# Second MLP's last quarter as seven half products with the final norm at its blocks, and the sum of four weight blocks built by loads in the lone steps

## Chip, core and metric

The kernel runs on one core of one Trainium2 chip. The time is in device microseconds (us), the median of several executions of the whole program. The engines are TensorE (PE), VectorE (DVE), ScalarE (ACT), GpSimd (POOL) and SyncE (SP). SP and POOL here mostly issue DMA transfers, each in the order of its own queue.

## What is computed

A trunk of two layers for 512 tokens with 1024 features. Each layer is a token mixer and a squared-ReLU MLP, and a last RMSNorm follows:

```
def sq_relu_mlp(h, w_up, w_down):
    return jnp.square(jax.nn.relu(h @ w_up)) @ w_down
...
    for i in range(DEPTH):
        h = rms_norm(x, norm_mix[i])
...
        h = rms_norm(x, norm_ffn[i])
        x = x + sq_relu_mlp(h, ffn_w_up[i], ffn_w_down[i])
    return rms_norm(x, final_norm)
```

`w_up` is 1024x4096 and `w_down` 4096x1024, all in float32.

## The kernel before

**The products.** A float32 product is made of three matmuls with operands split in two parts, high and low (`mm3`): high by high, high by low, low by high. The high part is a cast on ACT (L125), the low part a subtraction on DVE (L122). In the listings `wh` and `wl` are the two parts of a weight block (512x512), and a left operand is a pair of tiles `q`.

**The MLP.** `ffn` runs the hidden width in four quarters, c = 0 to 3. `up(c)` makes the squared hidden values of a quarter, four tiles `a11`, `a12`, `a21`, `a22` (`sq`). `down(c, sq)` multiplies them by the four blocks of `w_down` and adds the result to `x`. Either is a 2x2 product of blocks done by Winograd's scheme: seven half products instead of eight, each with a sum of weight blocks on one side. So one of `down`'s items has 2 x 4 x 3 = 24 matmuls with 512 columns, for the two 128-row blocks b = 0 and 1 of its half of the tokens. The items stand in a list `work` of pairs (prepare, go). `go` issues the matmuls of an item and then adds the two blocks to `x` on DVE (`accumulate`, L1155). `prepare` brings the weights, splits them and splits the left operand. The loop calls `prepare` of item j + 2 after `go` of item j. `up(c)` and `down(c - 1)` alternate, item by item. The last quarter has no partner: in the first MLP its seven items, `down(3)`, run by themselves. These are the **lone steps**, here numbered 1 to 7 as they run. Steps 1, 5, 6 and 7 use one pair of PSUM banks (X), and steps 5, 6 and 7 follow one another there. Since each adds to what the one before left, a block of step 6 or 7 can't start before DVE has read that bank.

**Weights of a lone step.** Six slots (`raws`) hold raw weight blocks. SP loads a block, and POOL adds another one to it during a transfer (`add`, L990, `accum_op`). With W00, W01, W10, W11 for the blocks of the last quarter, slot f has W00 for step 1, a has W01 + W00 for step 3, c has W10 for step 2, b has W11 for step 4. DVE then makes a = a + b for step 5 (`t2`, L1264). After that POOL adds W01 to b, which is the weight of step 6 (`p3`), and W10 to a, the sum of four, which is that of step 7 (`p4`).

**The end of the second MLP.** It gets `last_products` as `last`, and `down(3)` is not used. The four weight blocks are loaded and split whole, and eight plain half products follow (`block`, 24 matmuls each; the last one as two with 256 columns). After a block, DVE adds it to `x` (L1819), ACT sums the squares (L1823), DVE and POOL make the inverse root (L1829, L1837). For row blocks 0 to 2 `finish` scales the row of 1024 (L1842) and SP writes it out. For block 3 the product with the norm's gain is made ahead (L1862), and its two halves are scaled on DVE (L1867) and ACT (L1868).

A scheduler fixes the order of each engine's instructions when the program is built. On the chip each engine runs its own list in order and waits on semaphores.

Of the kernel before, what the change touches and what calls it, by code (L numbers as in the profile page):

```python
# [10 lines left out]
F32 = mybir.dt.float32  # L11
F32R = mybir.dt.float32r
# [5 lines left out]
P = 128  # L18
T = 512
NT = T // P  # L20
# [37 lines left out]
def trunk(ctx: ExitStack, tc: tile.TileContext, a):  # L58
# [10 lines left out]
    def nm(s):  # L69
        count[0] += 1  # L70
        return f"{s}_{count[0]}"
# [3 lines left out]
    def psum():  # L75
        if fixed[0] is not None:
            return fixed[0]()
        return psp.tile([P, T], F32, tag="ps", name=nm("ps"))
# [11 lines left out]
    def raw_tile(shape, name="wr"):  # L90
        return wp.tile(list(shape), F32, tag="wr", name=nm(name), bufs=2)
# [14 lines left out]
    def mm3(out, l, r, start, stop, terms=(0, 1, 2), **kw):  # L106
        (lh, ll), (rh, rl) = l, r
        for t in terms:
            lhsT, rhs = ((lh, rh), (lh, rl), (ll, rh))[t]
            nc.tensor.matmul(  # L110
                out, lhsT=lhsT, rhs=rhs, start=start and t == 0, stop=stop and t == 2, **kw
            )

    def gpair(t=None):

        if t is None:
            t = gxp.tile([P, 4, T // 2], F32R, tag="g", name=nm("g"))
        t = t.rearrange("p k n -> p (k n)")
        return t[:, 0:T], t[:, T : 2 * T]
# [4 lines left out]
    def split(hl, src, eng=None):  # L124
        nc.scalar.copy(hl[0], src)  # L125
        low(eng or nc.vector, hl[1], src, hl[0])
        return hl
# [20 lines left out]
    def wtiles(n1, n2, shift=0):  # L148

        return tuple(  # L150
            wp.tile([P, 2112], F32R, tag=t, name=nm(t))[:, shift : shift + n1 * n2].rearrange(
                "p (k c) -> p k c", k=n1
            )
            for t in ("wh", "wl")
        )
# [7 lines left out]
    def wview(w, r0, rows, c0, cols):  # L163
        return w[r0 : r0 + rows, c0 : c0 + cols].rearrange("(k p) c -> p k c", p=P)
# [87 lines left out]
    class Norm:  # L252
# [7 lines left out]
        def add(self, i, u):  # L260

            if u != self.late:
                self.square(i, u)
            else:
                self.left.append((i, u))
# [24 lines left out]
    def four(dtype=F32R):  # L290
        return gxp.tile([P, 4, H], dtype, tag="g", name=nm("g"))
# [697 lines left out]
    def add(t, src):  # L989
        nc.gpsimd.dma_start(t, src, accum_op=ALU.add)  # L990

    def ffn(layer, xq, norm, pool, after=None, last=None, mid=None):

# [162 lines left out]
        def down(c, sq):  # L1159
# [3 lines left out]
            def w(k, u):  # L1163
                return wview(w_dn, c * 1024 + k * 512, 512, u * 512, 512)
# [30 lines left out]
                return "a"  # L1195

            def p3():
                add(s["b"], w(0, 1))
                return "b"

            def p4():
                add(s["a"], w(1, 0))
                return "a"

            def n1():
                sq["n1"] = squares.get()
# [55 lines left out]

            def t2():
                nc.vector.tensor_add(s["a"], s["a"], s["b"])  # L1264

            return [
                item(lambda: "a11", w11, "X", True, (0, 0, r2, False), alone),
                item(lambda: "a12", w21, "Z", True, (0, 0, r2, True), True),
                item(n1, p1, "Y", True, (1, 1, nr2, False)),
                item(s4, w22, "Y", False, (0, 1, nr2, False), False, True, t2),  # L1270
                item(lambda: "a11", p2, "X", False, (0, 1, nr2, True), False, True),
                item(lambda: "a21", p3, "X", False, (1, 1, nr2, True), True, True),
                item(
                    lambda: "a22", p4, "X", False, (1, 0, r2, True), True, True,
# [8 lines left out]
                work += [p, q]  # L1283
            sq = new
        n_mixed = len(work)
        if last is None:
            work += down(3, sq)
        ahead = 2
        for prepare, _ in work[:ahead]:
            prepare()  # L1290
        for j, (_, go) in enumerate(work):
# [6 lines left out]
            go()  # L1298
            if j + ahead < len(work):
                work[j + ahead][0]()  # L1300
        if last is not None:
            spare[:] = banks
            last(
                r2,
                [
                    split(
                        (four(), four()) if n < 2 else tuple(
                            pool.tile([P, 4, H], F32R, tag="q", name=nm("q"), bufs=4)
                            for _ in range(2)
                        ), sq[t],  # L1310
                    )
                    for n, t in enumerate(("a11", "a12", "a21", "a22"))
                ],
            )
        fixed[0] = None


    norm1 = Norm(0)
    gx1 = Quarters("norm_mix", KD, 1)
    with stage(1), tc.tile_pool(name="ffn0", bufs=1) as fp:  # L1320
        ffn(0, gx0, norm, fp, norm1.add, None, gx1.first)

# [460 lines left out]
    with stage(1), tc.tile_pool(name="ffn1", bufs=1) as fp:  # L1785
        out = a["out"].rearrange("b (i p) d -> p (b i) d", p=P)

        def last_products(r2, quarters):
            w_dn = a["ffn_w_down"][1]
            ws = {}  # L1790
            gb = four(F32).rearrange("p k n -> p (k n)")
            for u in range(2):
                for kh in range(2):
                    raw = raw_tile((P, 4, 512))
                    nc.sync.dma_start(raw, wview(w_dn, 3 * 1024 + kh * 512, 512, u * 512, 512))
                    if u + kh < 2:
                        wh, wl = split(wtiles(4, 512), raw)
                        parts = [(wh[:, k, :], wl[:, k, :]) for k in range(4)]
                    else:
                        parts = [split(gpair(G6[k]), raw[:, k, :]) for k in range(4)]  # L1800
                    for k in range(4):
                        ws[u, kh * 4 + k] = parts[k]

            nc.sync.dma_start(gb, a["final_norm"].partition_broadcast(P))
            ssum = fp.tile([P, 16, 4], F32, name="ssum")

            def block(i, c0, cols, e):

                ps = psum()[:, 0:cols]
                bs = slice(i % 2 * P, (i % 2 + 1) * P)  # L1810
                u, w0 = c0 // 512, c0 % 512
                for k in range(8):
                    h, l = quarters[i // 2 * 2 + k // 4]
                    mm3(
                        ps, (h[:, k % 4, bs], l[:, k % 4, bs]),
                        tuple(t[:, w0 : w0 + cols] for t in ws[u, k]), k == 0, k == 7,
                    )
                yy = x[:, i, c0 : c0 + cols]
                nc.vector.scalar_tensor_tensor(  # L1819
                    out=yy, in0=ps, scalar=r2[:, i : i + 1], in1=yy, op0=ALU.mult, op1=ALU.add  # L1820
                )
                junk = tmp()
                nc.scalar.activation(  # L1823
                    junk[:, 0:cols], yy, AF.Square, accum_out=ssum[:, i, e : e + 1]
                )

            def mean(i, e, rest):
                m = small(1)
                nc.vector.tensor_scalar(  # L1829
                    out=m, in0=ssum[:, i, e : e + 1], scalar1=1.0 / D, scalar2=rest,  # L1830
                    op0=ALU.mult, op1=ALU.add,
                )
                return m

            def inverse(m):
                r = small(1)
                nc.gpsimd.tensor_tensor(out=r, in0=m, in1=mhalf[:, 0:1], op=ALU.pow)  # L1837
                return r

            def finish(i):  # L1840
                r = inverse(mean(i, 1, mean(i, 0, EPS)))
                nc.vector.scalar_tensor_tensor(  # L1842
                    out=x[:, i, :], in0=x[:, i, :], scalar=r, in1=gb, op0=ALU.mult, op1=ALU.mult,
                )
                nc.sync.dma_start(out[:, i, :], x[:, i, :])

            for i in range(0, 2):
                block(i, 0, 512, 0)
            for i in range(0, 2):
                block(i, 512, 512, 1)  # L1850
                finish(i)
            block(2, 0, 512, 0)
            block(2, 512, 512, 1)
            finish(2)

            i = NT - 1
            z = gpair(four(F32))
            m = EPS
            for e, (c0, cols) in enumerate(((0, 512), (512, 256), (768, 256))):
                block(i, c0, cols, e)  # L1860
                m = mean(i, e, m)
                nc.vector.tensor_mul(  # L1862
                    z[c0 // 512][:, c0 % 512 : c0 % 512 + cols], x[:, i, c0 : c0 + cols],
                    gb[:, c0 : c0 + cols],
                )
            r = inverse(m)
            nc.vector.tensor_scalar(out=z[1], in0=z[1], scalar1=r, scalar2=None, op0=ALU.mult)  # L1867
            nc.scalar.activation(z[0], z[0], AF.Copy, scale=r)  # L1868
            for uo in (1, 0):
                nc.sync.dma_start(out[:, i, uo * 512 : (uo + 1) * 512], z[uo])  # L1870

        ffn(1, gx2, norm2, fp, None, last_products)


_INS = [
# [22 lines left out]
```

## Time and profile before

| | us |
|---|---|
| median of 3 runs | 1098.06 (1094.0 to 1098.29) |
| the profiled execution's own time | 1092.22 |
| its span, first to last instruction | 1090.5 |
| TensorE busy in the span | 1058.8 |
| mean granted clock of TensorE, share of 2.4 GHz | 0.989 |

The span is cut from the profiled execution. Its own time is 1.72 us longer and stands 5.84 us under the median of the runs. Times in the rows below are us from the span's start.

### The profile page before, as it was taken

What the parts mean: (1) busy time and instruction counts of PE and PEld (TensorE: products, weight loads), DVE (VectorE), ACT (ScalarE), POOL (GpSimd) and SP (SyncE); (2) the same over time, 40 slices, a digit from 0 to 9 for tenths busy, and PEclk for the clock granted to TensorE, in tenths of its full rate; (3) what the DMA queues carried; (4) which work ended last, traced back from release to release, by engine and by line L of the source; (5) the groups of instructions that cost most, each with busy time, mean ns of one, the idle gap of its engine ahead of it and who ended that gap; (6) DMA issues with size and microseconds to landing.
All of it is one profiled execution on the core that took longest, in us unless ns stands there. A gap on an engine that the chain in (4) does not pass through costs nothing.

```text
span 1090.5 us, 15740 instructions
## 1 busy us (share of the span) xinstructions
PE 1058.8 (97%) x6540; PEld 947.4 (87%) x6540; DVE 864.3 (79%) x959; ACT 627.8 (58%) x712; POOL 115.4 (11%) x143
## 2 busy tenths in 40 slices
PE   8989999899999999989999999999999999999997
PEld 6778889899999999877788999887999899999986
DVE  6888866887887887887968588997988788888753
ACT  4567546665655655556755645556765555656531
POOL 5100000001001001002011000010001001001000
PEclk9989999999999999999999999999999999999999
DMA  6120246768768669447486836876686886757421
GB/s 204 39 79 2 76 117 197 204 142 174 212 144 186 178 149 199 149 78 175 139 161 141 231 85 193 237 134 181 156 222 125 218 194 125 225 115 119 120 109 59
DMA packets 86083, 163.33 MB, mean 150 GB/s; under 512 B 4917, under 2 KB 10620, under 8 KB 85884
## 3 DMA queue, kind: packets, MB, share of 16 engines
q0 software_dynamic: 33584, 67.11, 35.3%
q1 hardware_dynamic: 52428, 95.22, 25.4%
q8 instruction: 51, 0.84, 0.3%
q14 instruction: 20, 0.16, 0.0%
HBM read 160.22 MB, written 2.10 MB: 149 GB/s over the span
## 4 chain that ended last, share of the span: by engine, by line
PE 79%; DVE 8%; DMA 4%; issue 4%; ACT 4%; SPq 0%; POOL 0%; POOLq 0%; ACTq 0%; DVEq 0%
PE ps L110 74%; DVE wl L122 3%; ACT wh L125 2%; DMA wb<-in_sgu_w_in 2%; DMA wb<-in_ffn_w_down 1%; DVE g L122 1%; PE ps L1613 1%; PE ps L852 1%; DMA wb<-in_ffn_w_up 1%; PE ps L296 1%; PE ps L819 0%; PE ps L820 0%; PE ps L821 0%; PE ps L823 0%; PE ps L822 0%
## 5 line engine op out<-in xcount | busy, mean ns | idle before, releaser
L110 PE MATMUL ps<-g,wh 128*128 128x256 f32 (+1 forms) x2304 | 420.5, 285 | 9.0 <-DVE g L122 5.0
L110 PEld LDWEIGHTS ps<-g,wh 128*128 128x128 f32 x2304 | 359.9, 190 | 17.2 <-DVE g L122 5.9
L110 PE MATMUL ps<-g,wl 128*128 128x256 f32 (+1 forms) x1152 | 327.1, 284 | 0.6 <-DVE wl L122 0.6
L110 PE MATMUL ps<-wh,q 128*128 128x512 f32 (+1 forms) x840 | 266.5, 390 | 2.9 <-DVE x L1155 2.9
L122 DVE TENSOR_TENSOR wl<-wb,wh 128x2048 fp32r<-128x2048 f32 x75 | 171.7, 2289 | 68.8 <-ACT wh L125 68.8
L110 PEld LDWEIGHTS ps<-g,wl 128*128 128x128 f32 x1152 | 217.4, 189 | 2.2 <-DVE wl L122 0.9
L125 ACT CAST wh<-wb 128x2048 fp32r<-128x2048 f32 x75 | 143.0, 1907 | 119.5 <-PE ps L110 92.0
L110 PEld LDWEIGHTS ps<-wh,q 128*128 128x128 f32 x840 | 158.1, 189 | 34.9 <-issue 3.3
L122 DVE TENSOR_TENSOR wl<-wr,wh 128x2048 fp32r<-128x2048 f32 (+1 forms) x69 | 153.3, 2225 | 38.5 <-ACT wh L125 38.4
L125 ACT CAST wh<-wr 128x2048 fp32r<-128x2048 f32 (+1 forms) x69 | 127.8, 1855 | 64.2 <-PE ps L110 44.8
L110 PE MATMUL ps<-wl,q 128*128 128x512 f32 (+1 forms) x420 | 163.7, 390 | 0.0
L110 PE MATMUL ps<-wh,g 128*128 128x512 f32 x496 | 157.5, 395 | 1.9 <-DVE g L122 1.3
L110 PEld LDWEIGHTS ps<-wh,g 128*128 128x128 f32 x496 | 93.8, 189 | 23.3 <-DVE g L122 1.7
L125 ACT CAST q<-sq 128x1024 fp32r<-128x1024 f32 x51 | 53.6, 1051 | 90.4 <-PE ps L110 87.8
L110 PE MATMUL ps<-wl,g 128*128 128x512 f32 x248 | 97.7, 394 | 1.7 <-DVE wl L122 1.7
L110 PEld LDWEIGHTS ps<-wl,q 128*128 128x128 f32 x420 | 79.5, 189 | 14.5
L1155 DVE SCALAR_TENSOR_TENSOR x<-ps,s,x 128x512 f32<-128x512 f32 x98 | 72.6, 746 | 20.9 <-PE ps L110 20.9
L122 DVE TENSOR_TENSOR q<-sq,q 128x1024 fp32r<-128x1024 f32 x51 | 62.4, 1223 | 5.3 <-ACT q L125 2.3
L110 PEld LDWEIGHTS ps<-wl,g 128*128 128x128 f32 x248 | 46.9, 189 | 12.5 <-DVE wl L122 2.5
L990 POOL DMA_DIRECT2D wr<-in_ffn_w_up x16 | 20.9, 1308 | 268.9 <-DMA wr<-in_ffn_w_up 84.9
L990 POOL DMA_DIRECT2D wb<-in_ffn_w_down x17 | 21.9, 1291 | 133.8 <-DVE wl L122 131.6
L1072 DVE TENSOR_TENSOR sq<-sq,ps 128x512 f32<-128x512 f32 x48 | 32.6, 681 | 3.9 <-PE ps L110 2.6
(267 smaller groups left out, 1276.2 us busy)
## 6 DMA issues: line engine op xcount, KB each, us to landing
wb<-in_ffn_w_up SPq DMA_DIRECT2D x18, 1024.0 KB, 5.7
wb<-in_ffn_w_down SPq DMA_DIRECT2D x18, 1024.0 KB, 5.1
wb<-in_ffn_w_down POOLq DMA_DIRECT2D x17, 1024.0 KB, 9.4
wr<-in_ffn_w_up POOLq DMA_DIRECT2D x16, 1024.0 KB, 8.5
wr<-in_ffn_w_up SPq DMA_DIRECT2D x14, 1024.0 KB, 5.5
wr<-in_sgu_w_in POOLq DMA_DIRECT2D x9, 1024.0 KB, 10.4
wr<-in_ffn_w_down SPq DMA_DIRECT2D x8, 1024.0 KB, 5.1
wb<-in_ffn_w_up POOLq DMA_DIRECT2D x8, 1024.0 KB, 8.6
```

What stands on the lines that cost most here:

```text
L110: nc.tensor.matmul(out, lhsT=lhsT, rhs=rhs, start=start and t == 0, stop=stop and t == 2, **kw)
L122: return eng.tensor_sub(l, src, h.bitcast(F32))
L125: nc.scalar.copy(hl[0], src)
L296: nc.tensor.transpose(ps[:, i * P : (i + 1) * P], x[:, i, k * P : (k + 1) * P], ident)
L852: nc.tensor.transpose(ps[b][:, c : c + P], pr[h, i][:, j * P : (j + 1) * P], ident)
L990: nc.gpsimd.dma_start(t, src, accum_op=ALU.add)
L1072: both(name, lambda t, j: nc.vector.tensor_add(t, t, pv(acc[sums][j])))
L1155: nc.vector.scalar_tensor_tensor(out=xs, in0=ps, scalar=r[:, i : i + 1], in1=xs, op0=ALU.mult, op1=ALU.add)
L1613: nc.tensor.matmul(ps[:, i * P : (i + 1) * P], lhsT=m[:, i, :], rhs=wt[:, j // 2, :], start=True, stop=True,)
```

## The change

The second MLP now uses `down(3)` too, so its last quarter is seven lone steps with 168 matmuls of 512 columns where there were 168 of 512 and 48 of 256. The final norm (`normalised`) is called as `after(i, u)`, behind each block that has got its last addend. Half a row's sum of squares is taken as soon as that half is there, and the other half and the scaling follow with the second. The gain is loaded at the end of SP's list of the mixed part.

In the lone steps of both MLPs the sum of four is no longer made from a. Slot f, free after step 1's split, gets three adds: W01, W10 and W11. The weight of step 6 is loaded afresh into a slot g (W11) and W01 added to it, so b is given back after `t2`, and a after step 5.

```diff
             def p3():
-                add(s["b"], w(0, 1))
-                return "b"
+                if alone:
+                    fetch("g", 1, 1)
+                name = "g" if alone else "b"
+                add(s[name], w(0, 1))
+                return name
 
             def p4():
+                if alone:
+                    return "f"
                 add(s["a"], w(1, 0))
                 return "a"
+
+            def sums(k, u):
+
+                return (lambda: add(s["f"], w(k, u))) if alone else None
...
             def t2():
                 nc.vector.tensor_add(s["a"], s["a"], s["b"])
+                if alone:
+                    raws.put(s.pop("b"))
+                    add(s["f"], w(1, 1))
 
             return [
-                item(lambda: "a11", w11, "X", True, (0, 0, r2, False), alone),
-                item(lambda: "a12", w21, "Z", True, (0, 0, r2, True), True),
+                item(lambda: "a11", w11, "X", True, (0, 0, r2, False), late=sums(0, 1)),
+                item(lambda: "a12", w21, "Z", True, (0, 0, r2, True), True, late=sums(1, 0)),
                 item(n1, p1, "Y", True, (1, 1, nr2, False)),
                 item(s4, w22, "Y", False, (0, 1, nr2, False), False, True, t2),
-                item(lambda: "a11", p2, "X", False, (0, 1, nr2, True), False, True),
+                item(lambda: "a11", p2, "X", False, (0, 1, nr2, True), alone, True),
                 item(lambda: "a21", p3, "X", False, (1, 1, nr2, True), True, True),
...
-        if last is None:
-            work += down(3, sq)
+        work += down(3, sq)
...
+        def normalised(i, u):
+
+            if not gb:
+                gb.extend(four(F32).rearrange("p k n -> p (k n)") for _ in range(2))
+                nc.sync.dma_start(gb[0], a["final_norm"].partition_broadcast(P))
+            us = slice(u * 512, (u + 1) * 512)
+            junk = tmp()
+            nc.scalar.activation(junk, x[:, i, us], AF.Square, accum_out=ssum[:, i, u : u + 1])
+            z = gb[1][:, us] if i == NT - 1 else None
+            if (i, u) == (NT - 1, 1):
+                nc.vector.tensor_mul(z, x[:, i, us], gb[0][:, us])
+            first = 0 if i < 2 else 1
+            m = small(1)
+            nc.vector.tensor_scalar(
+                out=m, in0=ssum[:, i, u : u + 1], scalar1=1.0 / D,
+                scalar2=EPS if u == first else half[i], op0=ALU.mult, op1=ALU.add,
+            )
+            half[i] = m
+            if u == first:
+                return
+            r = small(1)
+            nc.gpsimd.tensor_tensor(out=r, in0=m, in1=mhalf[:, 0:1], op=ALU.pow)
+            if z is None:
                 nc.vector.scalar_tensor_tensor(
-                    out=yy, in0=ps, scalar=r2[:, i : i + 1], in1=yy, op0=ALU.mult, op1=ALU.add
+                    out=x[:, i, :], in0=x[:, i, :], scalar=r, in1=gb[0], op0=ALU.mult, op1=ALU.mult,
                 )
...
+            nc.scalar.activation(gb[1][:, 512:], gb[1][:, 512:], AF.Copy, scale=r)
+            nc.vector.scalar_tensor_tensor(
+                out=z, in0=x[:, i, us], scalar=r, in1=gb[0][:, us], op0=ALU.mult, op1=ALU.mult,
+            )
...
+        ffn(1, gx2, norm2, fp, normalised)
```

**POOL's queue in the first MLP's lone steps.** `wb_2044` is slot f, `wb_2042` a, `wb_2043` c and later g, `wb_2041` b. Before:

```order
L990 DMA wr_2039<-in_ffn_w_down 128x4x512
L990 DMA wb_2042<-in_ffn_w_down 128x4x512
L990 DMA wb_2041<-in_ffn_w_down 128x4x512
L990 DMA wb_2042<-in_ffn_w_down 128x4x512
L990 DMA wr_4742<-in_sgu_w_in 128x4x512
L990 DMA wr_4743<-in_sgu_w_in 128x4x512
```

And now:

```order
L990 DMA wr_2039<-in_ffn_w_down 128x4x512
L990 DMA wb_2042<-in_ffn_w_down 128x4x512
L990 DMA wb_2044<-in_ffn_w_down 128x4x512 x2
L990 DMA wb_2043<-in_ffn_w_down 128x4x512
L990 DMA wb_2044<-in_ffn_w_down 128x4x512
L990 DMA wr_4745<-in_sgu_w_in 128x4x512
L990 DMA wr_4746<-in_sgu_w_in 128x4x512
```

The two late adds to b and a are gone. In their place stand two adds to f, the add to g, and the third add to f behind it. The second MLP has the same order.

**DVE in the second MLP, from the split of step 7's weight on.** `x<-ps` is the addition of a block to `x`, L1800 a mean, L1810 the scaling of a row of 1024, `q_9333` step 7's left operand. There was no such part before. Now:

```order
L122 TENSOR_TENSOR wl_9337<-wb_6723,wh_9336 128x2048
L1800 TENSOR_SCALAR s_9317<-ssum,s_9200 128x1
L1154 SCALAR_TENSOR_TENSOR x<-ps_6736,s_6717,x 128x512
L1810 SCALAR_TENSOR_TENSOR x<-x,s_9319,g_9195 128x1024
L1800 TENSOR_SCALAR s_9326<-ssum,s_9205 128x1
L122 TENSOR_TENSOR q_9333<-sq_6727,q_9332 128x1024
L1810 SCALAR_TENSOR_TENSOR x<-x,s_9328,g_9195 128x1024
L1154 SCALAR_TENSOR_TENSOR x<-ps_6735,s_6717,x 128x512
L1154 SCALAR_TENSOR_TENSOR x<-ps_6736,s_6717,x 128x512
```

The first `x<-ps_6736` reads step 5's second block, the last two rows step 6's two. Both scalings stand ahead of the read of step 6's first block, for which step 7 waits.

**DVE at the very end.** Before:

```order
L1819 SCALAR_TENSOR_TENSOR x<-ps_6734,s_6712,x 128x256
L1862 TENSOR_TENSOR g_9341<-x,g_9124 128x256
L1829 TENSOR_SCALAR s_9399<-ssum,s_9369 128x1
L1819 SCALAR_TENSOR_TENSOR x<-ps_6727,s_6712,x 128x256
L1862 TENSOR_TENSOR g_9341<-x,g_9124 128x256
L1829 TENSOR_SCALAR s_9429<-ssum,s_9399 128x1
L1867 TENSOR_SCALAR g_9341<-g_9341,s_9432 128x512
```

And now:

```order
L1154 SCALAR_TENSOR_TENSOR x<-ps_6735,s_6716,x 128x512
L1800 TENSOR_SCALAR s_9402<-ssum,s_9367 128x1
L1810 SCALAR_TENSOR_TENSOR x<-x,s_9404,g_9195 128x1024
L1154 SCALAR_TENSOR_TENSOR x<-ps_6736,s_6716,x 128x512
L1800 TENSOR_SCALAR s_9411<-ssum,s_9373 128x1
L1817 SCALAR_TENSOR_TENSOR g_9196<-x,s_9413,g_9195 128x512
```

Row block 2 now ends only half a step ahead of block 3, and its scaling stands ahead of block 3's addition to `x`.

## Rows read from the trace of the kernel before

**Rows 1.** The page's first part: busy us (share of the span) xinstructions.

```profile
PE 1058.8 (97%) x6540; PEld 947.4 (87%) x6540; DVE 864.3 (79%) x959; ACT 627.8 (58%) x712; POOL 115.4 (11%) x143
```

**Rows 2.** Windows: length, busy PE, PEld, DVE, ACT, POOL, granted clock, DMA share, GB/s.

```profile
465.00:475.00 10.00, 10.00 (x46) 8.28 (x45) 10.00 (x9) 4.19 (x4) 1.28 (x1) 1.00 0.15 19
475.00:484.20 9.20, 9.20 (x42) 7.41 (x40) 4.33 (x5) 2.86 (x2) 1.30 (x1) 1.00 1.12 204
484.20:487.20 3.00, 0.16 (x1) 0.00 (x0) 2.89 (x4) 1.67 (x1) 0.00 (x0) 1.00 0.08 14
487.20:494.40 7.20, 7.16 (x25) 5.79 (x26) 6.94 (x5) 4.21 (x7) 0.25 (x1) 0.76 0.01 2
...
755.00:790.00 35.00, 32.09 (x249) 29.85 (x248) 30.87 (x33) 25.94 (x32) 2.58 (x2) 1.00 0.76 208
```

**Rows 3.** Timeline of PE: start, us, operation, [idle before <- releaser].

```profile
483.97 0.39 PE L110 MATMUL ps<-wh,q 128*128 128x512 f32 x1
487.24 0.77 PE L110 MATMUL ps<-wh,q 128*128 128x512 f32 x1 [2.88 <-DVE x L1155]
...
494.37 0.49 PE L296 MATMUL ps<-ident,x 128*128 128x128 f32 x3
```

**Rows 4.** Timeline of POOL in the lone steps.

```profile
471.43 1.28 POOL L990 DMA_DIRECT2D wb<-in_ffn_w_down  x1 [43.79 <-DVE wl L122]
475.42 1.30 POOL L990 DMA_DIRECT2D wb<-in_ffn_w_down  x1 [2.71 <-DVE wl L122]
```

**Rows 5.** Timeline of ACT there.

```profile
480.40 1.91 ACT L125 CAST wh<-wb 128x2048 fp32r<-128x2048 f32 x1 [6.00 <-DMA wb<-in_ffn_w_down]
...
485.53 1.90 ACT L125 CAST wh<-wb 128x2048 fp32r<-128x2048 f32 x1 [2.26 <-DMA wb<-in_ffn_w_down]
```

**Rows 6.** Timeline of DVE there.

```profile
449.36 2.29 DVE L122 TENSOR_TENSOR wl<-wb,wh 128x2048 fp32r<-128x2048 f32 x1
...
475.60 1.21 DVE L122 TENSOR_TENSOR q<-sq,q 128x1024 fp32r<-128x1024 f32 x1
476.73 0.74 DVE L1155 SCALAR_TENSOR_TENSOR x<-ps,s,x 128x512 f32<-128x512 f32 x1
482.35 2.29 DVE L122 TENSOR_TENSOR wl<-wb,wh 128x2048 fp32r<-128x2048 f32 x1 [4.87 <-ACT wh L125]
```

**Rows 7.** The chain that ended last, behind the first MLP.

```profile
501.27 0.70 PE ps L110 x3
...
501.99 8.43 DMA wb<-in_sgu_w_in
```

**Rows 8.** The page's DMA queues: packets, MB, share of 16 engines.

```profile
q0 software_dynamic: 33584, 67.11, 35.3%
q1 hardware_dynamic: 52428, 95.22, 25.4%
```

**Rows 9.** Timeline of DVE at the end of the program.

```profile
1072.41 0.75 DVE L1819 SCALAR_TENSOR_TENSOR x<-ps,s,x 128x512 f32<-128x512 f32 x1 [3.69 <-PE ps L110]
1074.02 0.21 DVE L1829 TENSOR_SCALAR s<-ssum,s 128x1 f32<-128x1 f32 x1 [0.85 <-ACT t L1823]
1074.88 1.28 DVE L1842 SCALAR_TENSOR_TENSOR x<-x,s,g 128x1024 f32<-128x1024 f32 x1 [0.65 <-POOL s L1837]
1077.86 0.75 DVE L1819 SCALAR_TENSOR_TENSOR x<-ps,s,x 128x512 f32<-128x512 f32 x1 [1.69 <-PE ps L110]
...
1083.61 0.48 DVE L1819 SCALAR_TENSOR_TENSOR x<-ps,s,x 128x256 f32<-128x256 f32 x1 [1.54 <-PE ps L110]
```

**Rows 10.** Timeline of ACT at the end.

```profile
1084.18 0.42 ACT L1823 ACTIVATE t<-x 128x256 f32<-128x256 f32 x1 [2.36 <-DVE x L1819]
...
1085.59 0.72 ACT L1868 ACTIVATE g<-g,s 128x512 f32<-128x512 f32 x1 [0.90 <-POOL s L1837]
```

**Rows 11.** Timeline of SP at the end.

```profile
1086.11 0.81 SPq L1870 DMA_DIRECT2D out<-g  x2
```

**Rows 12.** Windows of the eight plain products, columns as above.

```profile
1050.00:1060.00 10.00, 10.00 (x46) 8.29 (x45) 3.06 (x5) 1.45 (x4) 0.56 (x1) 1.00 0.00 0
```

More of the change, by code (lines that the diff above doesn't have):

```diff
@@ L990, in add, with ffn @@
         nc.gpsimd.dma_start(t, src, accum_op=ALU.add)
-    def ffn(layer, xq, norm, pool, after=None, last=None, mid=None):
+    def ffn(layer, xq, norm, pool, after=None, mid=None):
         w_up, w_dn = a["ffn_w_up"][layer], a["ffn_w_down"][layer]
@@ L1300, in ffn @@
                 work[j + ahead][0]()
[L1301 to L1314, printed above, removed]
         fixed[0] = None
@@ L1320, in trunk @@
     with stage(1), tc.tile_pool(name="ffn0", bufs=1) as fp:
-        ffn(0, gx0, norm, fp, norm1.add, None, gx1.first)
+        ffn(0, gx0, norm, fp, norm1.add, gx1.first)
     norm2 = Norm(0)
@@ L1786, in trunk @@
         out = a["out"].rearrange("b (i p) d -> p (b i) d", p=P)
[L1788 to L1818, printed above, removed]
-                nc.vector.scalar_tensor_tensor(
-                    out=yy, in0=ps, scalar=r2[:, i : i + 1], in1=yy, op0=ALU.mult, op1=ALU.add
[L1821 to L1843, printed above, removed]
@@ new lines, in trunk @@
+        gb = []
+        ssum = fp.tile([P, 16, 4], F32, name="ssum")
+        def normalised(i, u):
[20 more added lines that the diff above has]
+            if z is None:
+                nc.vector.scalar_tensor_tensor(
+                    out=x[:, i, :], in0=x[:, i, :], scalar=r, in1=gb[0], op0=ALU.mult, op1=ALU.mult,
@@ L1844, in finish @@
                 )
                 nc.sync.dma_start(out[:, i, :], x[:, i, :])
[L1847 to L1864, printed above, removed]
-                )
@@ L1866, in last_products @@
[L1866 to L1872, printed above, removed]
+                return
+            nc.scalar.activation(gb[1][:, 512:], gb[1][:, 512:], AF.Copy, scale=r)
+            nc.vector.scalar_tensor_tensor(
+                out=z, in0=x[:, i, us], scalar=r, in1=gb[0][:, us], op0=ALU.mult, op1=ALU.mult,
+            )
@@ L1875 @@
+            for uo in (1, 0):
+                nc.sync.dma_start(
+                    out[:, i, uo * 512 : (uo + 1) * 512], gb[1][:, uo * 512 : (uo + 1) * 512]
+                )
+        half = {}
+        ffn(1, gx2, norm2, fp, normalised)
 _INS = [
```

## The prediction

> **What bounds the kernel now.** I read the page's busy times first. TensorE is busy for 1058.8 of 1090.5 us [rows 1], so only two things help: fewer matmuls, or one of its few stalls taken away. The change touches both, so I went to its two places, the lone steps of the first MLP (they end at 501.97 us, [rows 7]) and the last quarter of the second (1040 us to the end).
>
> In the lone steps of the first MLP PE runs without a gap until step 5 ends, then idles [rows 2, 3]. Its last matmul of step 5 starts at 483.97. At the pace of a block, 24 matmuls in 5.45 us (1072.41 to 1077.86, [rows 9]) or 0.227 us each, step 6 would have started at 484.20. It starts at 487.24, 3.04 us late. After the idle stretch the granted clock is at its lower level, 1.2 GHz, for a part of step 6 (mean 0.76 over 487.20 to 494.40, [rows 2]), and step 6 takes 7.13 us, from 487.24 to the transposes at 494.37, instead of 5.45. That is another 1.68.
>
> The row names a DVE addition to `x` as releaser, but the cause lies further back. DVE idled 4.87 us before the split of step 6's weight at 482.35, for ACT's cast [rows 6], and ACT waited 6.00 us for the add of POOL [rows 5]. POOL issued it at 471.43 [rows 4] and the cast began at 480.40, 8.97 later. The second late add went out at 475.42 and its cast began at 485.53, 10.11 later, with the two sharing DMA engines that were full (share 1.12, [rows 2]). So the first MLP loses 3.04 + 1.68 = 4.72 us because two adds can be issued only after b and a have had their last other use.
>
> In the second MLP the eight plain products keep PE busy without a gap [rows 12], DVE and ACT are mostly idle (3.06 and 1.45 of 10 us), and the program ends with a short chain on DVE, ACT, POOL and SP.
>
> **First MLP.** Step 6's weight no longer needs b. Slot g takes c's tile, so its load may go right after step 2's split, early in the lone steps, and the add to it when that has landed. The sum of four starts once f is split, at 449.36 + 2.29 = 451.65 [rows 6], with three adds, each waiting for the one before to land. DVE's work stays the same in number and order, and where it idled for 4.87 us it now has its operands. So the 4.72 are gained, if f lands in time. Step 7 would start at 484.20 + 5.45 = 489.65, and its weight needs a cast of 1.91 and a split of 2.29 [rows 5, 6] ahead of it: f is due at 485.4.
>
> When does it land? An add alone is 8.97 from issue to cast, an overlapped one 10.11. Three in a row give 451.65 + 26.9 = 478.6, or 482.0. The add to g stands in POOL's queue ahead of f's third, and it and the load of g use the same engines. The queue of adds took 35.3% of 1090.5 us for 67.11 MB, 6.0 us per block of 1.05 MB, and SP's 25.4% for 95.22 MB, 3.1 us per block [rows 8]. Those 3.1 come on top where g's load falls beside f's first add, which would be 484 at most with overlapped adds, rounded down because they share. I take 481.5, and 478.6 to 484 as bounds, so f is in time in the first MLP by 1.4 to 6.8 us. If the cover (steps 3 to 6 on PE) were gone, step 7 would wait by f's lateness.
>
> What follows the first MLP moves with it: the next load that PE waits on is issued at 501.99, right behind the last matmul at 501.97 [rows 7]. So I count 4.72 in full.
>
> **Second MLP, matmuls.** Seven steps of 5.45 replace seven plain products of 5.45 and one of 5.75 (1077.86 to 1083.61, its last columns in halves, [rows 9]): 5.75 us less. The added work ahead of it, sums of hidden tiles and of weights on DVE, is what the first MLP's lone steps have too, and there PE had no gap up to step 5 with DVE busy 10.00 of 10 us [rows 2]. The load of the gain stands in SP's list among the loads of the mixed part and costs no engine anything.
>
> At this place a figure of the Trainium skill speaks against the size. "TensorE: Matmul & The Clock Gate", section Back-to-back issue gap, gives some 131 ns per matmul of 512 columns in a stream of weight loads and matmuls. By it the 24 matmuls would be worth 3.1 us. The row has 227 ns here, and the sum goes by that.
>
> **Second MLP, step 7.** Here the norm adds work to a DVE that has no room. From the end of step 5's first block, 2.72 before step 6 starts (call that T), DVE does in order: addition to `x` 0.75, split of f 2.29, mean 0.21, addition 0.75, scaling 1.28, mean 0.21, split of q 1.21, scaling 1.28, addition 0.75. That is 8.73, and 8.1 as successive operations start some 0.08 early (475.60 + 1.21 against 476.73) [rows 6, 9]. It ends at T + 5.4, and step 7, which needs the last of them, is due at T + 5.45. There is no slack, so every wait in it goes to PE one for one. The first wait is f's cast: DVE can start f's split at T - 2.05, so f has to land by T - 4.0, 480.2 in the first MLP's times. With f at 481.5 step 7 starts 1.3 late. Bounds: 0 with f at 478.6, 3.8 with 484. Whether the clock falls after such a gap is open: it fell behind one of 2.88, while 2.9 us of idle time spread over 755 to 790 left it at 1.00 [rows 2]. I take no loss for 1.3, and 1.7 more at the upper bound.
>
> **The tail.** Row block 2 used to be done two products before the end. Now it ends 2.72 ahead of PE's last matmul (call that E). From its addition to its scaling are 2.47 (1072.41 to 1074.88), so the scaling runs from E - 0.23 to E + 1.05, and block 3's addition to `x`, behind it on DVE, starts at E + 0.97 instead of at once. Its own chain works on 512 columns, 2.47 again, where 256 took 1.98 (1083.61 to 1085.59 [rows 9, 10]): 0.49 more. The first write then follows ACT's scaling of 0.72 or DVE's of 0.75, where it followed the faster one at 1086.11 [rows 10, 11], 0.52 behind it: 0.2 more. Together 1.66, so 1.6; bounds 0.7 (no collision) and 2.
>
> **Sum.** -4.72 - 5.75 + 1.3 + 1.6 = -7.6 us. The profiled execution's 1092.22 becomes 1084.6. The runs shown have a median 5.84 above it; on that the sum gives 1090.5. I say **1090**.
>
> **Rivals.**
> (1) *The adds run one behind the other and step 7 waits in both MLPs: slower.* The mechanism is the chain of adds into f with g's add in front of its last link. With four in series at 10.11, f lands at 492.1. Step 7 is then 6.7 late in the first MLP and 11.9 in the second, and the clock falls for 1.7 each time: -4.72 + 8.4 - 5.75 + 13.6 + 1.6 = +13.1, 1111 on the median. It decides from f at 486.4 on, where the lateness eats all (6.2 and 1.0 late, one fall of the clock). For it speaks the DMA share of 1.12 with only two adds; against it that those two landed 5.1 apart and not 9 or 10, so adds overlap. Chance 0.08.
> (2) *f lands at 484 and the clock falls in the second MLP:* 3.8 + 1.7 instead of 1.3, so -3.4, 1094.7. Chance 0.14.
> (3) *The first half doesn't do what it says:* step 6 of the first MLP still waits, for DVE's queue. Then -2.9, 1095.2. The idle 4.87 us on DVE speak against it. Chance 0.06.
> (4) *POOL can't issue its adds while DVE is busy.* If each of the four adds waits for a running split of 2.29, f lands 6.9 to 9.2 later than its earliest 478.6, at 485.5 to 487.8, about the point where (1) decides: +1, 1099. The issues took 1.28 and 1.30 [rows 4], the first of them inside a stretch with DVE busy 10.00 of 10 [rows 2]. Chance 0.03.
> The Trainium skill has a rule for this last one, in "SBUF — State Buffer", section SBUF: two separate sides: DVE in some modes locks GpSimd out of a shared port, and transfers issued by GpSimd wait for their descriptors. By that rule (4) would hold; the trace of before does not show it.
>
> **How the numbers follow.** The forecast, with f between 478.6 and about 483, has 0.69. Its own range is -9.5 to -5.5, 1088.5 to 1092.5 on the median. The base itself is loose, 1092.22 to 1098.29 over the executions shown, and on the profiled one's base the forecast is 1083 to 1087. The range reaches from there to case (3): 1083 to 1096. What can be told from no change is 0.5%, 5.5 us. Faster by more: the forecast, less its weak end, 0.68. Within: (2), (3) and that end, 0.23. Slower: (1) and half of (4), 0.09.
>
> **What the profile after would show.** Right: no gap of PE before step 6 of the first MLP, the clock at 1.00 there, and the load behind that MLP issued 4.7 earlier; 48 matmul instructions fewer; in the second MLP a gap of 0 to 3.8 before step 7, released by an addition to `x`, with a scaling just ahead of that on DVE; about 8.5 us from PE's last matmul to the span's end, where 6.9 are now. Wrong: casts of f that begin later than 485 in the first MLP's present times, a new wait of ACT for the add to g, or gaps ahead of steps 1 to 5 in the second MLP.

## The result and the profile after

The changed kernel takes 1086.3 us (median of 7 runs, 1085.58 to 1090.41), the kernel before, run beside it, 1094.16 (7 runs, 1092.15 to 1102.05). The ratio is 0.9925 with a 95% interval of 0.9904 to 0.9946: faster by some 8 us. The forecast was 1090 and faster. The profiled execution took 1085.58 us, with a span of 1083.9 and a mean granted clock of 0.991.

The page's busy times, against [rows 1]:

```profile
PE 1051.2 (97%) x6492; PEld 940.5 (87%) x6492; DVE 883.2 (81%) x969; ACT 637.1 (59%) x713; POOL 125.7 (12%) x150
```

TensorE has 48 instructions and 7.6 us less, DVE 18.9 us more, and that did not make DVE the bound.

**First MLP.** Windows of the stretch up to step 6, and of the one in which step 6 used to wait and run (columns as in [rows 2]):

```profile
475.00:484.20 9.20, 9.20 (x42) 7.60 (x42) 8.99 (x9) 5.63 (x5) 0.00 (x0) 1.00 0.52 95
484.20:492.00 7.80, 7.71 (x36) 6.20 (x35) 6.14 (x7) 5.50 (x6) 1.28 (x1) 1.00 0.00 1
```

PE is busy for all but 0.09 us of the two, and the clock stays at its upper level, 2.4 GHz, where [rows 2] had a mean of 0.76. POOL's timeline shows the four adds: f, f, g, f.

```profile
452.21 1.28 POOL L990 DMA_DIRECT2D wb<-in_ffn_w_down  x1 [24.35 <-DVE wl L122]
461.01 1.30 POOL L990 DMA_DIRECT2D wb<-in_ffn_w_down  x1 [7.52 <-DMA wb<-in_ffn_w_down]
465.11 1.29 POOL L990 DMA_DIRECT2D wb<-in_ffn_w_down  x1 [2.79 <-DMA wb<-in_ffn_w_down]
470.48 1.28 POOL L990 DMA_DIRECT2D wb<-in_ffn_w_down  x1 [4.08 <-DMA wb<-in_ffn_w_down]
```

ACT's casts of g and of f, in its timeline:

```profile
475.31 1.92 ACT L125 CAST wh<-wb 128x2048 fp32r<-128x2048 f32 x1 [0.75 <-DMA wb<-in_ffn_w_down]
478.88 1.06 ACT L125 CAST q<-sq 128x1024 fp32r<-128x1024 f32 x1 [1.65 <-PE ps L110]
480.15 1.92 ACT L125 CAST wh<-wb 128x2048 fp32r<-128x2048 f32 x1 [0.21 <-DMA wb<-in_ffn_w_down]
```

ACT waited for both slots, for 0.75 and 0.21 us where [rows 5] had 6.00 and 2.26, and PE waited for neither. The three links of f took 8.80, 9.47 and 9.67 us (461.01 - 452.21, 470.48 - 461.01, 480.15 - 470.48). The first load behind this MLP, in the chain that ended last:

```profile
497.61 8.76 DMA wb<-in_sgu_w_in
```

It is 4.38 earlier than in [rows 7], though the split of f, with which the lone steps' loads begin, stood 0.16 later than in [rows 6] (DVE's timeline):

```profile
449.52 2.29 DVE L122 TENSOR_TENSOR wl<-wb,wh 128x2048 fp32r<-128x2048 f32 x1
```

**Second MLP.** The one wait of PE there, in its timeline:

```profile
1069.84 0.47 PE L110 MATMUL ps<-wh,q 128*128 128x512 f32 x1 [0.78 <-DVE x L1154]
```

It is step 7's first matmul. Step 6's last one starts at 1068.68, so 1068.91 was due, and 0.93 us are lost. The windows of 1066 to 1072 have the clock at 1.00, so no fall is added to that. DVE's timeline shows why:

```profile
1061.66 2.29 DVE L122 TENSOR_TENSOR wl<-wb,wh 128x2048 fp32r<-128x2048 f32 x1
1063.87 0.21 DVE L1800 TENSOR_SCALAR s<-ssum,s 128x1 f32<-128x1 f32 x1
1063.99 0.74 DVE L1154 SCALAR_TENSOR_TENSOR x<-ps,s,x 128x512 f32<-128x512 f32 x1
1064.76 1.28 DVE L1810 SCALAR_TENSOR_TENSOR x<-x,s,g 128x1024 f32<-128x1024 f32 x1
1065.96 0.21 DVE L1800 TENSOR_SCALAR s<-ssum,s 128x1 f32<-128x1 f32 x1
1066.09 1.22 DVE L122 TENSOR_TENSOR q<-sq,q 128x1024 fp32r<-128x1024 f32 x1
1067.75 1.28 DVE L1810 SCALAR_TENSOR_TENSOR x<-x,s,g 128x1024 f32<-128x1024 f32 x1 [0.45 <-POOL s L1808]
1068.95 1.41 DVE L1154 SCALAR_TENSOR_TENSOR x<-ps,s,x 128x512 f32<-128x512 f32 x2
```

This is the queue that the prediction wrote down, op for op. With step 6 starting at 1068.91 - 5.45 = 1063.46, f's split could have started at 1061.41, and began 0.25 later, for f's cast. Another 0.45 is a wait for the inverse root on POOL, which took 1.46 us instead of 0.56 (last section). The remaining 0.23 is the hand-over between these engines and PE.

**The tail.** PE's last row, DVE's last scaling of 1024 with block 3's addition and last scaling, and SP's last write, in three timelines:

```profile
1075.16 0.39 PE L110 MATMUL ps<-wh,q 128*128 128x512 f32 x1
```

```profile
1075.34 1.29 DVE L1810 SCALAR_TENSOR_TENSOR x<-x,s,g 128x1024 f32<-128x1024 f32 x1 [0.65 <-POOL s L1808]
1076.54 0.74 DVE L1154 SCALAR_TENSOR_TENSOR x<-ps,s,x 128x512 f32<-128x512 f32 x1
...
1079.01 0.75 DVE L1817 SCALAR_TENSOR_TENSOR g<-x,s,g 128x512 f32<-128x512 f32 x1 [0.66 <-POOL s L1808]
```

```profile
1079.76 0.81 SPq L1821 DMA_DIRECT2D out<-g  x2
```

PE ends at 1075.55, block 3's addition starts 0.99 behind it, and the span ends 8.32 behind it (6.95 before).

**Where the time went, by section.** The span is cut at four marks that every kernel here has: A, the split of f (449.36 in [rows 6], 449.52 above); B, the first load behind the first MLP (501.99 in [rows 7], 497.61); C, ACT's read of a hidden tile as the last quarter's lone steps of the second MLP begin, which stands in the timelines of before and of the changed kernel as

```profile
1031.48 0.60 ACT L1101 ACTIVATE sq<-ps 128x512 f32<-128x512 f32 x1
```

```profile
1028.14 0.60 ACT L1100 ACTIVATE sq<-ps 128x512 f32<-128x512 f32 x1 [0.19 <-PE ps L110]
```

and E, the end of PE's last matmul (1083.57 before: its last twelve start at 1081.97 and take 1.60). Differences, in us, of one profiled execution each, the experiments below included:

| kernel | A to B, first MLP | B to C, mixer and on | C to E, second MLP | E to the end |
|---|---|---|---|---|
| before | 52.63 | 529.49 | 52.09 | 6.95 |
| changed | 48.09 | 530.53 | 47.41 | 8.32 |
| both_again | 48.07 | 532.31 | 47.34 | 8.27 |
| loads_alone | 48.14 | 533.40 | 52.09 | 6.87 |
| halves_alone | 52.14 | 532.29 | 52.09 | 8.61 |
| fresh_g_alone | 50.81 | 533.47 | 51.10 | 8.42 |
| one_more_add | 59.77 | 533.71 | 58.82 | 8.37 |
| scalings_behind | 48.07 | 531.29 | 46.34 | 8.30 |
| norm_out_of_the_way | 48.10 | 531.49 | 46.34 | 7.35 |

For the changed kernel: -4.54 + 1.04 - 4.68 + 1.37, and 0.16 ahead of A, are the -6.65 between the two spans. A itself stands between 447.46 (fresh_g_alone) and 452.95 (halves_alone), though the work ahead of it is the same in all of them. So single executions differ by several us where no edit reaches, and B to C is such a place too. Only the first MLP, the second and the end are read as effects of an edit below.

### The profile page after: what moved, and what is told of

The parts are those of the page before. It is cut to its first block, busy times and chain, and to the rows that moved or that the text cites. A ratio compares the mean times of both kernels' runs of the same rounds, so it can differ in the third digit from the quotient of the medians.

```text
span 1083.9 us, 15689 instructions
## 1 busy us (share of the span) xinstructions
PE 1051.2 (97%) x6492; PEld 940.5 (87%) x6492; DVE 883.2 (81%) x969; ACT 637.1 (59%) x713; POOL 125.7 (12%) x150
## 4 chain that ended last, share of the span: by engine, by line
PE 77%; DVE 9%; DMA 6%; issue 4%; ACT 3%; POOL 0%; SPq 0%; POOLq 0%; ACTq 0%; DVEq 0%
PE ps L110 72%; DMA wb<-in_ffn_w_down 3%; DVE wl L122 3%; DMA wb<-in_sgu_w_in 2%; ACT wh L125 2%; DVE g L122 1%; PE ps L1609 1%; PE ps L852 1%; DMA wb<-in_ffn_w_up 1%; DVE sq L485 1%; PE ps L296 1%; PE ps L819 0%; PE ps L820 0%; PE ps L823 0%; PE ps L821 0%
## 5 line engine op out<-in xcount | busy, mean ns | idle before, releaser
L110 PE MATMUL ps<-wh,q 128*128 128x512 f32 x896 | 284.1, 390 | 0.9 <-DVE x L1154 0.8
L122 DVE TENSOR_TENSOR wl<-wb,wh 128x2048 fp32r<-128x2048 f32 x82 | 187.7, 2290 | 66.3 <-ACT wh L125 66.3
L125 ACT CAST wh<-wb 128x2048 fp32r<-128x2048 f32 x82 | 156.7, 1910 | 116.9 <-PE ps L110 94.4
L110 PEld LDWEIGHTS ps<-wh,q 128*128 128x128 f32 x896 | 168.1, 188 | 35.6 <-issue 1.5
L110 PE MATMUL ps<-wl,q 128*128 128x512 f32 x448 | 174.9, 390 | 0.0
L110 PE MATMUL ps<-wh,g 128*128 128x512 f32 x448 | 142.4, 396 | 2.1 <-DVE g L122 1.3
L110 PEld LDWEIGHTS ps<-wh,g 128*128 128x128 f32 x448 | 84.7, 189 | 21.5 <-DVE g L122 1.7
L1154 DVE SCALAR_TENSOR_TENSOR x<-ps,s,x 128x512 f32<-128x512 f32 x112 | 82.9, 747 | 22.2 <-PE ps L110 22.1
L110 PE MATMUL ps<-wl,g 128*128 128x512 f32 x224 | 88.2, 394 | 1.8 <-DVE wl L122 1.8
L110 PEld LDWEIGHTS ps<-wl,g 128*128 128x128 f32 x224 | 42.4, 190 | 11.7 <-DVE wl L122 2.6
L990 POOL DMA_DIRECT2D wb<-in_ffn_w_down x24 | 31.0, 1290 | 165.6 <-DVE wl L122 132.4
```

Source lines behind the costliest of these rows:

```text
L110: nc.tensor.matmul(out, lhsT=lhsT, rhs=rhs, start=start and t == 0, stop=stop and t == 2, **kw)
L122: return eng.tensor_sub(l, src, h.bitcast(F32))
L1154: nc.vector.scalar_tensor_tensor(out=xs, in0=ps, scalar=r[:, i : i + 1], in1=xs, op0=ALU.mult, op1=ALU.add)
```

## The experiments

Two theories stand against each other. The first: the sum of four built by loads is what removes the waits, in both MLPs, so the seven products would wait without it. The second: each half of the change earns its own term of the sum, whatever becomes of the other.

**loads_alone** and **halves_alone**: one half of the change each. The first is the kernel before with the added lines of `p3`, `p4`, `sums`, `t2` and the items; its second MLP keeps the eight products. The second is the changed kernel with these lines taken out:

```diff
             def p3():
-                if alone:
-                    fetch("g", 1, 1)
-                name = "g" if alone else "b"
-                add(s[name], w(0, 1))
-                return name
+                add(s["b"], w(0, 1))
+                return "b"
...
-                    add(s["f"], w(1, 1))
```

> The lone steps' sums by loads alone in the first MLP; the second MLP's last quarter stays eight plain products. My theory: the gap ahead of step 6 (3.04 us) and the lower clock behind it (1.68) go, 4.4 to 4.7 us, ratio to before 0.9957 to 0.9960; the load behind the first MLP is issued 4.2 to 4.7 earlier, the program's end keeps its 6.9 us behind the last matmul. Rival, the first MLP's gain is given back in the mixer behind it: ratio 0.998 to 1.000. Rival, the two halves of the change add up: the rest to the change's 0.9925 is then about 3.5 us for the second half.

> Seven half products and the norm at their blocks in the second MLP, but the lone steps' weights of steps 6 and 7 by late adds to b and a, as before, in both MLPs. My theory: the second MLP then gets the stall that the first one has: 3.0 us of gap ahead of step 6 and 1.7 for the clock, on top of 5.75 saved in matmuls and 1.4 lost at the end, so about 0.4 us slower than before to 1 faster, ratio 0.999 to 1.001. Rival, the halves add up: the gain of both (8.2) less that of the loads (4.5), 3.5 us, ratio 0.9968. A third: step 7 waits as well behind the scalings on DVE, then 2 us more, ratio 1.002.

**both_again** is the changed kernel once more, on the same chip as these.

> The changed kernel as it is, for runs on the same chip as its parts. All theories: ratio to before 0.990 to 0.995.

Measured against 1095.3 (23 runs): loads_alone 1091.15 (12 runs), ratio 0.9963 (0.9945 to 0.9981); halves_alone 1099.15 (12 runs), 1.0027 (1.0008 to 1.0046); both_again 1086.88 (6 runs), 0.9921 (0.9899 to 0.9943). Of 1095 us the ratios make -4.1, +3.0 and -8.7 us. The halves don't add up: 7.6 us come only from having both, with some 2 us of uncertainty on each ratio. The table shows 4.75 of them in the second MLP; the first MLP and the end differ from a sum of the halves by 0.4 us or less, so the rest is not placed. In loads_alone the first MLP has the whole gain (48.14). In halves_alone the second MLP takes 52.09, what the eight products took: the 5.75 us of saved matmuls are all spent, on two waits and on the slower clock behind the first. PE's timeline there:

```profile
1075.24 0.47 PE L110 MATMUL ps<-wh,q 128*128 128x512 f32 x1 [2.40 <-DVE x L1154]
1083.77 0.47 PE L110 MATMUL ps<-wh,q 128*128 128x512 f32 x1 [1.20 <-DVE x L1154]
```

Behind the first wait the granted clock falls (0.66 in the windows of 1075 to 1080). Its cause, in ACT's timeline, is the same as in the first MLP of the kernel before [rows 5]:

```profile
1068.40 1.91 ACT L125 CAST wh<-wb 128x2048 fp32r<-128x2048 f32 x1 [5.58 <-DMA wb<-in_ffn_w_down]
1073.65 1.90 ACT L125 CAST wh<-wb 128x2048 fp32r<-128x2048 f32 x1 [2.39 <-DMA wb<-in_ffn_w_down]
```

The second wait is step 7's: the third case of the expectation came, in which step 7 waits as well. So the seven products pay here only with the loads changed, and the second theory falls.

**fresh_g_alone** divides the loads: g is loaded afresh, the sum of four is made from a as before.

```diff
             def p4():
-                if alone:
-                    return "f"
                 add(s["a"], w(1, 0))
                 return "a"
...
-                return (lambda: add(s["f"], w(k, u))) if alone else None
+                return None
```

> The changed kernel with the sum of four made as before, by a late addition to slot a once step 5's weight is split, and only slot g loaded afresh. It divides the first gain between the two slots. Theory: the gap of 3.04 us ahead of step 6 was slot g's, so it goes with g afresh; but the late sum in a comes near 484 and its split stands ahead of step 6's second block, which is then late by about 2.3 us in the first MLP and 3 to 4 us in the second: 5 to 6 us above the changed kernel, ratio about 0.9975. Rival: a fresh g gives everything and the late sum is hidden as it was before: the time of the changed kernel within 1 us, ratio 0.9925.

Measured: 1095.82 (10 runs) against 1094.72 (17 runs), ratio 1.0007 (0.9989 to 1.0024). The MLPs behave as the theory said: 2.7 and 3.7 us longer than in the changed kernel, by waits of 1.76 and 0.74 in the first and 2.16 and 0.69 in the second. The cast of the late slot a in ACT's timeline, and the first wait with the matmul ahead of it in PE's:

```profile
481.99 1.91 ACT L125 CAST wh<-wb 128x2048 fp32r<-128x2048 f32 x1 [4.11 <-DMA wb<-in_ffn_w_down]
```

```profile
484.78 0.39 PE L110 MATMUL ps<-wh,q 128*128 128x512 f32 x1
486.94 0.50 PE L110 MATMUL ps<-wh,q 128*128 128x512 f32 x1 [1.76 <-DVE x L1154]
```

The ratio was missed: 0.0082 above that of the changed kernel is 9 us, where the two MLPs explain 6.4. Another 2.9 are in the section from B to C, in which both_again, the same program as the changed kernel, took 1.8 more too. By the timing, one late add that is left takes back all that the change brings, though the sections don't place all of it on that add. The fresh slot g is not enough without the sum in f.

**one_more_add** prices a later f. The block of row 1, column 1 goes into the sum twice, so step 7's weight and the output are not the reference's.

```diff
                     raws.put(s.pop("b"))
                     add(s["f"], w(1, 1))
+                    add(s["f"], w(1, 1))
```

> The changed kernel with one more accumulating load into slot f in the lone steps of both MLPs (the block of row 1, column 1 added a second time, so the weight of step 7 is not the reference's). It prices a later slot f. Theory: the sum in f had no spare time: it landed about 480 in the first MLP and 1059.5 in the second, and a further load in series adds about 8.6 us, so f comes near 488.7 and 1068. f's second half of the split stands on VectorE ahead of the addition that step 6's second block waits for, so TensorE stops there for 6.5 to 7.5 us in each MLP, with a clock fall worth up to 1.7 us behind each: 14 to 18 us above the changed kernel, ratio to before 1.005 to 1.010. Rival: the loads have room and the fourth addition is hidden as the third was: under 3 us above the changed kernel, ratio under 0.996.

Measured: 1109.58 (4 runs) against 1094.72, ratio 1.0132 (1.0104 to 1.0161), 22.7 us above the changed kernel by the ratios, and 11.7 and 11.4 in the two MLPs. PE's timeline, with one wait in each:

```profile
497.09 0.79 PE L110 MATMUL ps<-wh,q 128*128 128x512 f32 x1 [8.97 <-DVE x L1154]
...
1091.84 0.80 PE L110 MATMUL ps<-wh,q 128*128 128x512 f32 x1 [9.76 <-DVE x L1154]
```

The first wait with what led to it, in the timelines of PE (the last matmul of step 6's first block), ACT and DVE:

```profile
487.73 0.39 PE L110 MATMUL ps<-wh,q 128*128 128x512 f32 x1
492.15 1.90 ACT L125 CAST wh<-wb 128x2048 fp32r<-128x2048 f32 x1 [11.33 <-DMA wb<-in_ffn_w_down]
494.08 2.29 DVE L122 TENSOR_TENSOR wl<-wb,wh 128x2048 fp32r<-128x2048 f32 x1 [9.59 <-ACT wh L125]
496.29 0.74 DVE L1154 SCALAR_TENSOR_TENSOR x<-ps,s,x 128x512 f32<-128x512 f32 x1
```

In DVE's list the split of f stands ahead of the addition of step 5's second block, and step 6's second block needs that addition. It was due at 487.73 + 0.23 = 487.96 and started at 497.09, 9.13 late. So a cast of f at 492.15 - 9.13 = 483.02 would have cost nothing: that is 32.6 behind mark A (450.40). fresh_g_alone agrees: step 6's second block was 486.94 - 485.01 = 1.93 late there, and 481.99 - 1.93 = 480.06 is 32.6 behind its A (447.46). In the changed kernel the cast of f came 30.6 behind A, in both_again 31.6 (481.76, A at 450.13), in loads_alone 31.9 (479.86, A at 447.99). So 0.7 to 2.0 us were left.

The sum in f has no room for another link, as the theory said, but the cost was undersized. The cast came 41.75 behind A, 11.1 later than in the changed kernel, where 8.6 was counted for the link; so the waits are 1.5 to 3.3 us longer than expected. And the clock stays at its lower level, 1.2 GHz, for longer behind them. The windows across the two waits, with the first 8 us of the first one by themselves:

```profile
488.00:504.00 16.00, 7.03 (x21) 5.47 (x21) 7.70 (x6) 7.26 (x8) 1.30 (x1) 0.68 0.26 44
488.00:496.00 8.00, 0.12 (x1) 0.00 (x0) 1.92 (x1) 3.85 (x5) 0.00 (x0) 0.80 0.37 68
1080.00:1097.00 17.00, 7.24 (x22) 5.33 (x21) 7.56 (x8) 4.34 (x7) 2.03 (x2) 0.70 0.41 93
```

A mean of 0.68 over 16 us is 10 us at half of the upper level. But the clock falls while PE still waits, and that part costs nothing. What the rest costs follows from the table: the first MLP is 11.7 longer with a wait of 9.1, so the slower matmuls cost 2.6 us, where 1.7 was the most that was counted.

**scalings_behind** asks what the 0.93 us at step 7 are. The scalings of blocks 0 and 1 go behind step 6's first addition, on DVE.

```diff
             if u == first:
+                if i == NT - 1:
+                    while later:
+                        later.pop(0)()
                 return
...
+                if i < 2:
+                    later.append(scale)
+                else:
+                    scale()
```

> The changed kernel with one edit: the final norm's scalings of blocks 0 and 1 are issued behind step 6's first addition to x instead of ahead of it; the tail (block 2 whole on VectorE, then block 3) stays as changed. Theory: the 0.93 us that step 7's first matmul stands late in the changed kernel is VectorE's queue (the scaling of block 1 ahead of the addition) alone, so the gap goes and the tail stays at about 8.4 us behind TensorE's last matmul: 0.8 us less than the changed kernel, 1085.5 where that is 1086.3, ratio to before about 0.9915. Rival: step 7 is late for its weight slot, which this doesn't touch; then the gap stays at 0.8 us or over and the time is that of the changed kernel within 0.3 us.

Measured: 1088.42 (6 runs) against 1094.72, ratio 0.9933 (0.9908 to 0.9957). PE waits nowhere in the second MLP, which takes 46.34: 1.07 less than in the changed kernel and 5.75 less than before. f's split is no earlier, so slot f was not what held step 7; DVE's queue was. The time itself doesn't show it: 0.8 us is inside the interval.

**norm_out_of_the_way** does the same, and also scales block 2 in two halves, on ACT and DVE, DVE's behind block 3's addition.

```diff
+            if (i, u) == (NT - 2, 1):
+                nc.vector.tensor_mul(x[:, i, us], x[:, i, us], gb[0][:, us])
...
+                if i < 2:
+                    later.append(scale)
+                else:
+                    nc.scalar.activation(x[:, i, 512:], x[:, i, 512:], AF.Copy, scale=r)
+                    later.append(half_scale)
```

> The changed kernel with the scalings of blocks 0 and 1 put behind step 6's first addition, and block 2 scaled in two halves: one on ACT, one on DVE behind block 3's addition to x. My theory: the gap of 0.78 us ahead of step 7 goes (0.9 us of matmul time), and the chain from PE's last matmul to the span's end shortens by 0.9, from 8.35 to about 7.4: 1.8 us faster than the changed kernel, ratio to before lower by 0.0017. Rival, the gap is that of the weight f (ACT waited 0.65 for its add) and not of the scalings: the gap stays at 0.5 to 0.8 and only the end gains, 0.9. Rival, the end is set by the writes: nothing gained there.

Measured: 1084.53 (5 runs) against 1095.3, ratio 0.9901 (0.9879 to 0.9923), the lowest here. The second MLP takes 46.34 again and the tail 7.35. DVE's timeline has block 3's addition right behind PE's last matmul and the scaling behind it:

```profile
1075.51 0.75 DVE L1156 SCALAR_TENSOR_TENSOR x<-ps,s,x 128x512 f32<-128x512 f32 x1 [0.90 <-PE ps L110]
1076.17 0.74 DVE L1827 SCALAR_TENSOR_TENSOR x<-x,s,g 128x512 f32<-128x512 f32 x1
```

Against both_again, on the same chip, the intervals overlap; that it beats the changed kernel is the traces' word (1.0 and 0.9 us in the sections touched), not the timing's.

## Why the prediction was right

The sum said -7.6 us; the medians have -7.9 and the two profiled spans -6.65. Term by term:

- **First MLP, -4.72:** measured -4.54. Both parts are as told: no wait, no fall of the clock. With one of the two late adds left it is -1.82 (fresh_g_alone).
- **Slot f at 481.5, bounds 478.6 to 484:** its cast began at 480.15, with all of the lone steps 0.16 later than before. The three links took 27.9 us in all, between three lone adds (26.9) and three overlapped ones (30.3).
- **When f is due in the first MLP:** here the prediction was wrong. It had 485.4, from the start of step 7, and so a margin of 1.4 to 6.8 us. But the split of f stands on DVE ahead of an addition that step 6's second block waits for; the prediction's own queue for the second MLP has it in that place. one_more_add and fresh_g_alone put the due time at 32.6 behind A, which is 482.0 in the times of before. So the margin was 0.7 to 2.0 us in the executions profiled, and f at the upper bound of 484 would have cost 2 us where nothing was counted. That the 4.72 came in full rests on an early f and not on the margin that was worked out. The point from which rival (1) decides, 486.4, is too late for the same reason.
- **Second MLP, matmuls -5.75:** where nothing waits (scalings_behind, norm_out_of_the_way) 46.34 against 52.09 is -5.75. So the rows' times held (5.45 us for a product of 24 matmuls, or 227 ns each, and 5.75 for the one with halved columns). The Trainium skill has 131 ns in "TensorE: Matmul & The Clock Gate", section Back-to-back issue gap; the rows here don't agree with it.
- **Step 7, +1.3:** measured 0.93 late and 1.07 in the section. The queue and its lack of slack were right, the source only partly: the sum had all of it from a late f. f was late by 0.25 there, 0.45 was POOL's inverse root, and 0.23 the hand-over between them and PE; the sum had the last two at nothing. That the size came out near is in part luck. That the clock would stay up behind it was right.
- **Tail, +1.6:** +1.37, with block 3's addition 0.99 behind PE's end where 0.97 was worked out.
- **What the sum left out:** it counted the load behind the first MLP and took all that follows as fixed. The section from B to C took 1.04 us more in the changed kernel's execution, which came to 1085.58 where the sum gave 1084.6. But both_again, the same kernel, took 2.82 more there and the other experiments 1.80 to 4.22, and the execution of before that all are measured against lies 1.9 us under its median. Whether the change gives back anything in that section is not shown.
- **The base:** 1098.06 for before was a median of three. Over the 7, 23 and 17 runs since, it was 1094.16, 1095.3 and 1094.72, so the sum's 1090.5 stood on a base some 3 to 4 us too high; from 1094.16 it gives 1086.6. That is why 1086.3 lies below the forecast's own range on the median (1088.5 to 1092.5), though inside the whole one (1083 to 1096).

Of the rivals, (1) and (2) need f later than it came; one_more_add shows (1) as a mechanism, with 23 us above the changed kernel once f is a link later. (3) did not happen. Against (4), POOL's issues took 1.28 to 1.30 us with DVE nearly full (18.35 of 20 us from 452 to 472), and the links of f are no longer than adds that share the engines, so no wait of that kind shows. The rule that the prediction named, in the Trainium skill's "SBUF — State Buffer", section SBUF: two separate sides, speaks of DVE's two-port modes and says that `tensor_tensor`, the operation of the splits, has none; so it does not make (4) hold, as the prediction had it.

**The section from B to C.** Part of what the executions differ by here comes from the clock's fall behind the first MLP, and from where it stands. Windows of the changed kernel, and then of scalings_behind:

```profile
512.00:522.00 10.00, 7.46 (x25) 5.57 (x24) 10.00 (x9) 8.48 (x8) 0.00 (x0) 0.83 0.58 191
522.00:532.00 10.00, 9.53 (x42) 7.90 (x43) 10.00 (x11) 6.98 (x8) 0.00 (x0) 1.00 0.63 223
```

```profile
512.00:522.00 10.00, 5.73 (x24) 4.43 (x24) 10.00 (x8) 8.76 (x8) 0.00 (x0) 1.00 0.59 191
522.00:532.00 10.00, 9.86 (x36) 8.04 (x37) 9.35 (x11) 5.46 (x7) 0.00 (x0) 0.83 0.64 221
```

At 522 PE waits for a split on DVE, which is busy 10.00 of 10 us. In the changed kernel the clock falls ahead of that wait, and the slower matmuls only shorten it:

```profile
522.48 0.50 PE L110 MATMUL ps<-wl,g 128*128 128x512 f32 x1 [1.75 <-DVE wl L122]
```

In scalings_behind it falls behind the wait, which is then longer, and the slower matmuls are lost time:

```profile
522.14 0.50 PE L110 MATMUL ps<-wl,g 128*128 128x512 f32 x1 [3.31 <-DVE wl L122]
```

That is worth 3.31 - 1.75 = 1.56 us. The executions of loads_alone, halves_alone and one_more_add have the long wait too, those of before, both_again and norm_out_of_the_way the short one, and fresh_g_alone has both falls (0.83 in both windows). So this much goes with the execution, not with the edit, and it is no part of the changed kernel's 1.04, since before has the short wait too. The rest of this section's differences, up to 2.8 us, lies mostly between 600 and 820 us; its cause stays open.

## What to carry to other kernels

Saving matmuls pays only if the operands of the steps that remain come as early as the steps: here the same 5.75 us were gained or fully lost by when two sums of weights could start. A chain of adding loads should start from a slot that is free early, and its links be counted one by one against whatever stands behind its use in an engine's list, which can be needed sooner than the sum itself; one link too many cost 23 us. And where an engine's queue has no slack, what nobody waits for (a final scaling) goes behind what TensorE waits for.

## What the runs showed of the hardware

**A tiny operation on POOL waits for DVE.** The inverse root has one element per partition. POOL's timeline of the changed kernel:

```profile
1064.16 0.56 POOL L1808 TENSOR_TENSOR s<-s,G 128x1 f32<-128x1 f32 x1 [13.35 <-DVE s L1800]
1066.25 1.46 POOL L1808 TENSOR_TENSOR s<-s,G 128x1 f32<-128x1 f32 x1 [1.52 <-DVE s L1800]
1074.76 0.54 POOL L1808 TENSOR_TENSOR s<-s,G 128x1 f32<-128x1 f32 x1 [7.05 <-DVE s L1800]
```

The first ran beside DVE's addition from PSUM (1063.99), the third beside nothing, the second beside the subtraction for `q` (1066.09 to 1067.31), both of whose inputs are in SBUF, and it ended 0.40 behind that. All seven executions profiled with the seven products have one such long root, 1.46 to 1.53 us, beside a DVE operation with two inputs in SBUF; none beside an addition from PSUM alone took over 0.57. The Trainium skill, "GPSIMD Engine Reference", section Specifications, says that GpSimd shares its way into SBUF with VectorE and that they collide when a VectorE instruction has two SBUF inputs. These rows agree, but in all seven the long root is also the second of two that follow one another, and no run here changed DVE's operation to test it by itself.

**Idle time and the clock.** A wait of 2.59 us in the first MLP of halves_alone left the clock at 1.00 (windows of 484 to 500), one of 2.40 in its second MLP was followed by a fall, one of 2.16 in the second MLP of fresh_g_alone too (0.57 in the windows of 1073 to 1077), and one of 2.88 in the kernel before as well [rows 2, 3]. Two shorter ones, 1.76 and 0.74, in the first MLP of fresh_g_alone were not. So the length of a wait alone did not tell whether its loss would double.
